# Squared-ReLU MLP by seven products: where the factors' differences, one weight sum and the last pair's stores are made

## The chip, the cores and the metric

The kernel runs on one core of a Trainium2 chip. The metric is device time of one launch in microseconds (us), lower is better; the time of a kernel is the median of its runs. The engines are named as the profile names them: PE (TensorE, matmuls), DVE (VectorE), ACT (ScalarE), POOL (GpSimd) and SP (SyncE, which only issues DMAs here). Each takes its instructions in the order of the program that was built; an instruction whose input isn't ready holds what is behind it on its engine.

## The reference

One layer on x (512 × 2048, float32): RMSNorm, a combined projection, stick-breaking attention and a gated branch, a merge, then the MLP, to which everything here belongs:

```
x = x + out
x = x + W2 relu(W1 RMSNorm(x))^2      # W1: 2048 x 8192, W2: 8192 x 2048
```

The result is float32 and is compared as such. The kernel makes a float32 product of three matmuls: each factor is split into a high part (hi, a cast by ACT) and the rest (lo = source − hi, a subtraction by DVE), and hi·hi, hi·lo and lo·hi are added in PSUM (`mm3`, L71 to L73).

## The kernel before

**First product.** The normalised x, turned (x2T, 16 tiles of 128 × 512), meets W1 in 32 pairs of 2 × 128 hidden columns. Pairs 0 and 1 are plain (`PLAIN = 2`). Pairs 2 to 31 take two blocks of columns, two halves of the tokens and two halves of the contraction as 2 × 2 blocks, and make seven products in place of eight (`NAMES` = y11, y21, m7, m6, y22, m4, m5, in this order). The seven factors of the activation side are x2T's own quarters (y11, y21, y22) and the differences m7 = y12 − y22, m6 = m7 − y11, m4 = y21 + m6, m5 = y11 − y12, made for each of eight k by `factors` (L646 to L649) while pair 1 runs, each into a new tile `m`, then split (L106, L107) into tiles `ys`. The weight side's sums are made for each pair by `Sums` on DVE: L172 (m7: w11 + w21), L176 (m6: + w22), L178 (y22: w12 is added). m5's factor w21 + w22 is made by a DMA that GpSimd issues and that adds w22 from DRAM into w21 (L174). SP loads the four blocks, 512 KB each (L166). Each product has 24 matmuls of 128 × 256, each pair 168.

**Hidden values.** `keep_hidden` squares a pair's activations, makes the same four differences from them, splits the seven factors and stores them to DRAM (`store`, 256 KB each, L687, by SP). The two plain pairs and pair 2 are kept together behind pair 2, then one pair behind each pair.

**Second product.** Eight chunks f of four pairs; for each chunk two halves g of the output columns; in each half seven products of 2 × 12 matmuls of 128 × 512 (i = 0 and 1 are two sets of weight blocks with their own `Sums`). GpSimd fetches the factors back (`ys<-store`, L737) and the residual (x2, from `kept`, 16 tiles, L754). The result of each product is added to x2 by DVE (L768). The next chunk's factors are fetched in `between`, behind each product.

**What sets the order.** The program is written as above, and a scheduler that models the engines (a `TileContext` with `schedule_with_timeline_sim=True`) sets the order of each engine's instructions. Tiles come from pools: `slots` (64 tiles of 256 KB) for activations and factors, `raws` for weight blocks (6) with `more` (6) added for the second product, and `w_piece` (6) for hi and lo of weights, which is three products ahead. `issue_after` holds an instruction behind another one in the order. `behind` is a list of small tasks; `step()` runs the next of them, `flush()` the rest. GpSimd and SP have eight transfers each in flight: an issue waits for the one eight earlier to land.

## Time and profile before

| | |
|---|---|
| median of 3 runs | 2529.33 us (2528.76 to 2530.37) |
| profiled execution | 2529.15 us |
| its span in the profile | 2527.2 us |
| PE busy | 2486.2 us, 98% of the span |
| DVE busy | 1600.5 us, 63% |
| pairs 0 and 1, then pair 2 | pair 2 from 1271.06 to 1301.0 us |
| pairs 3 to 30 | 1301.0 to 1865.5 us |
| pair 31 and the second product | 1865.5 us to the last matmul's end at 2521.9 us |

A row of the timeline has the start in us, the duration, the engine, the line of the kernel, the operation, the written tile and the read ones, and in brackets the idle time of the engine ahead of it with what ended it. A row of the table of stretches has the bounds, their length, then for each engine the busy time with the number of instructions, the granted clock of TensorE (1.00 is full), the share of DMA time and GB/s. Rows of waits have: total us, times, longest.

### The profile page before, as it was taken

Reading aid. Unit: us, or ns where it says so; the run is one execution under the profiler, and the core shown is the slowest. Engines: PE = TensorE matmul, PEld = TensorE weight load, DVE = VectorE, ACT = ScalarE, POOL = GpSimd, SP = SyncE. Lnnn points to the kernel's source line nnn. Section 1 sums busy time; section 2 is a strip of 40 time slices with the busy share of each in tenths; the row PEclk is TensorE's granted clock in tenths of the full one; section 3 lists DMA queues with packets and bytes.
Section 4 is the critical chain, followed back from the end, with each engine's and each line's share of the span. In section 5 each row is a group of like instructions: output and inputs, shape, how many; then the busy total and the mean of one; then the engine's idle time right before and its main releaser. Section 6 shows DMA issues by size and latency. Waiting matters only on the chain.

```text
span 2527.2 us, 35103 instructions
## 1 busy us (share of the span) xinstructions
PE 2486.2 (98%) x13658; PEld 2170.2 (86%) x13658; DVE 1600.5 (63%) x2106; ACT 1036.0 (41%) x1510; POOL 336.7 (13%) x425
## 2 busy tenths in 40 slices
PE   8999999999999999999999999999988999999999
PEld 7888888888888888888889999999986888888887
DVE  4555463232335343332798888888877889889887
ACT  5333342222223322232466666666653333333333
POOL 0212110000121010100000000000033223222210
PEclk9999999999999999999999999999998999999999
DMA  5332322333433233344368888887899787777763
GB/s 175 92 84 75 92 67 92 100 96 97 117 93 108 92 96 120 117 158 125 85 185 220 229 227 223 220 223 214 221 313 332 248 257 248 223 215 221 248 183 94
DMA packets 324711, 418.62 MB, mean 166 GB/s; under 512 B 17040, under 2 KB 177856, under 8 KB 324544
## 3 DMA queue, kind: packets, MB, share of 16 engines
q1 hardware_dynamic: 265440, 320.94, 39.9%
q0 software_dynamic: 59104, 95.44, 15.9%
q8 instruction: 107, 1.75, 0.3%
q14 instruction: 60, 0.49, 0.1%
HBM read 349.20 MB, written 67.11 MB: 165 GB/s over the span
## 4 chain that ended last, share of the span: by engine, by line
PE 95%; DMA 2%; DVE 2%; issue 1%; ACT 1%; POOL 0%; SPq 0%; DVEq 0%; POOLq 0%; ACTq 0%
PE q L72 17%; PE q L71 17%; PE q L73 17%; PE xo L73 2%; PE xo L71 2%; PE xo L72 2%; PE gb L71 2%; PE gb L72 2%; PE gb L73 2%; PE ga L71 2%; PE ga L72 2%; PE ga L73 2%; DMA w_raw<-in_w_ff_dram 2%; PE v L71 1%; PE v L73 1%; PE v L72 1%
## 5 line engine op out<-in xcount | busy, mean ns | idle before, releaser
L106 ACT CAST w_hi<-w_raw 128x1024 fp32r<-128x1024 f32 x434 | 456.8, 1052 | 600.7 <-PE q L72 548.8
L95 DVE TENSOR_TENSOR w_lo<-w_raw,w_hi 128x1024 fp32r<-128x1024 f32 x216 | 268.1, 1241 | 597.2 <-ACT w_hi L93 593.0
L107 DVE TENSOR_TENSOR w_lo<-w_raw,w_hi 128x1024 fp32r<-128x1024 f32 x434 | 530.6, 1223 | 137.4 <-ACT w_hi L106 137.1
L93 ACT CAST w_hi<-w_raw 128x1024 fp32r<-128x1024 f32 x216 | 227.2, 1052 | 664.9 <-PE ga L72 99.6
L72 PE MATMUL q<-ys,w_hi 128*128 128x256 f32 x1680 | 476.4, 284 | 4.1 <-DVE ys L107 4.1
L73 PE MATMUL q<-ys,w_lo 128*128 128x256 f32 x1680 | 472.7, 284 | 6.4 <-DVE w_lo L107 6.4
L71 PE MATMUL q<-ys,w_hi 128*128 128x256 f32 x1680 | 476.7, 285 | 1.0 <-ACT ys L106 0.8
L72 PE MATMUL q<-w_lo,ys 128*128 128x512 f32 x896 | 351.3, 392 | 11.1 <-DVE w_lo L107 11.1
L73 PE MATMUL q<-w_hi,ys 128*128 128x512 f32 x896 | 350.8, 392 | 0.0
L72 PEld LDWEIGHTS q<-ys,w_hi 128*128 128x128 f32 x1680 | 324.5, 193 | 4.9 <-DVE ys L107 4.9
L73 PEld LDWEIGHTS q<-ys,w_lo 128*128 128x128 f32 x1680 | 322.4, 193 | 6.6 <-DVE w_lo L107 6.6
L71 PEld LDWEIGHTS q<-ys,w_hi 128*128 128x128 f32 x1680 | 324.5, 193 | 1.9 <-ACT ys L106 1.5
L71 PE MATMUL q<-w_hi,ys 128*128 128x512 f32 x896 | 315.3, 391 | 0.9 <-ACT w_hi L106 0.9
L72 PEld LDWEIGHTS q<-w_lo,ys 128*128 128x128 f32 x896 | 169.6, 189 | 47.5 <-DVE w_lo L107 12.2
L71 PEld LDWEIGHTS q<-w_hi,ys 128*128 128x128 f32 x896 | 169.5, 189 | 36.6 <-ACT w_hi L106 1.3
L73 PEld LDWEIGHTS q<-w_hi,ys 128*128 128x128 f32 x896 | 169.6, 189 | 35.4
L174 POOL DMA_DIRECT2D w_raw<-in_w_ff_dram x62 | 85.9, 1393 | 819.2 <-DVE w_raw L172 543.6
L768 DVE TENSOR_TENSOR x<-x,q 128x512 f32<-128x512 f32 x256 | 167.9, 682 | 9.0 <-PE q L73 7.3
L737 POOL DMA_DIRECT2D ys<-store x224 | 126.8, 599 | 208.0 <-PE q L73 173.1
L71 PE MATMUL xo<-w_hi,mT_hi 128*128 128x512 f32 x256 | 100.5, 393 | 0.0
L73 PE MATMUL xo<-w_hi,mT_lo 128*128 128x512 f32 x256 | 99.9, 391 | 0.0
L72 PE MATMUL xo<-w_lo,mT_hi 128*128 128x512 f32 x256 | 99.7, 389 | 0.0
(259 smaller groups left out, 4216.2 us busy)
## 6 DMA issues: line engine op xcount, KB each, us to landing
w_raw<-in_w_ff_dram SPq DMA_DIRECT2D x256, 512.0 KB, 5.2
w_raw<-in_w_in_dram SPq DMA_DIRECT2D x144, 512.0 KB, 3.8
store<-ys SPq DMA_DIRECT2D x224, 256.0 KB, 5.1
ys<-store POOLq DMA_DIRECT2D x224, 256.0 KB, 6.0
w_raw<-in_w_ff_dram POOLq DMA_DIRECT2D x62, 512.0 KB, 6.9
w_raw<-in_w_out_dram SPq DMA_DIRECT2D x32, 512.0 KB, 3.8
w_raw<-in_w_oa_dram SPq DMA_DIRECT2D x16, 512.0 KB, 3.7
w_raw<-in_w_ob_dram SPq DMA_DIRECT2D x16, 512.0 KB, 3.7
```

The lines of the kernel that those rows point to most:

```text
L71: nc.tensor.matmul(o, lhsT=lh[0], rhs=rh[0], start=start, stop=False, **kw)
L72: nc.tensor.matmul(o, lhsT=lh[0], rhs=rh[1], start=False, stop=False, **kw)
L73: nc.tensor.matmul(o, lhsT=lh[1], rhs=rh[0], start=False, stop=stop, **kw)
L93: nc.scalar.copy(out=hi, in_=raw)
L95: nc.vector.tensor_tensor(out=lo, in0=raw, in1=f32(hi), op=ALU.subtract)
L106: nc.scalar.copy(out=hi, in_=src)
L107: state["lo"] = nc.vector.tensor_tensor(out=lo, in0=src, in1=f32(hi), op=ALU.subtract)
L174: nc.gpsimd.dma_start(out=self.w21, in_=self.blocks[1, 1], accum_op=ALU.add)
L737: nc.gpsimd.dma_start(out=f32(t), in_=store[f][NAMES.index(name), p])
L768: nc.vector.tensor_tensor(out=a, in0=a, in1=o, op=op)
```

## The change

- `factors` becomes `factor`, which makes one kind of difference for one k, and writes it in place, into x2T's y22 (m7, m6, m4) or y12 (m5). Pair 1's four steps make m7 for all eight k, then m6 for all eight; m4 and m5 of the first k are made ahead of pair 2, those of the others as tasks in `behind`, two k at a time, behind the products of pair 2.
- The kept pairs: one behind pair 2, up to two behind each later pair until none is left over, in place of all at once.
- `Sums` has `loaded=False` for pair 31 and for chunk f = 0 (`strassen_tokens` with `loaded=f > 0`): w21 + w22 is then an addition on DVE (L181 in the new numbering) ahead of m5, and there is no accumulating DMA.
- The fetches of chunk 0 (L788 in the new numbering) and of x2 (L803) are written mixed: three factors ahead of the second product, the others behind its products, with two tiles of x2 at a time; the fetches of chunk 1 begin at the end of f = 0, g = 0.
- f = 0, g = 0 has its m7 sums held behind the last addition to pair 31's activations (`issue_after`).
- Pair 31's squares, differences, splits and stores are tasks of `behind` in f = 1 (`keeping`).

```diff
     class Sums:
-        def __init__(self, blocks, tiles):
-            self.blocks = blocks
+        def __init__(self, blocks, tiles, loaded=True):
+            self.blocks, self.loaded = blocks, loaded
...
         def parts(self, name):
...
                 nc.vector.tensor_tensor(out=self.a, in0=self.w11, in1=self.w21, op=ALU.add)
-                nc.gpsimd.dma_start(out=self.w21, in_=self.blocks[1, 1], accum_op=ALU.add)
+                if self.loaded:
+                    nc.gpsimd.dma_start(out=self.w21, in_=self.blocks[1, 1], accum_op=ALU.add)
...
                 nc.vector.tensor_tensor(out=self.w12, in0=self.c, in1=self.w12, op=ALU.add)
+            if name == "m5" and not self.loaded:
+                nc.vector.tensor_tensor(out=self.w21, in0=self.w21, in1=self.w22, op=ALU.add)
...
-    def strassen_columns(wap, c0, rhs, evac):
+    def strassen_columns(wap, c0, rhs, evac, loaded=True):
...
             evac(name, o)
+            step()
...
-    def strassen_tokens(wap, r0, c0, lhs, evac, between):
+            step()
+    def strassen_tokens(wap, r0, c0, lhs, evac, between, loaded=True, after=None):
...
             for i in range(2):
-                hi, lo = ws[i].parts(name)
+                with tc.issue_after(after.ins) if after and name == "m7" else nullcontext():
+                    hi, lo = ws[i].parts(name)
...
             between(name)
+            step()
...
 -    def factors(ys, act, k):
+    def factor(ys, act, k, name):
         y11, y12, y21, y22 = act[0][:, :HS], act[0][:, HS:], act[1][:, :HS], act[1][:, HS:]
-        ta, tb = slot("m"), slot("m")
-        m = {"m7": ta[:, :HS], "m6": ta[:, HS:], "m4": tb[:, :HS], "m5": tb[:, HS:]}
-        nc.vector.tensor_tensor(out=m["m7"], in0=y12, in1=y22, op=ALU.subtract)
-        nc.vector.tensor_tensor(out=m["m6"], in0=m["m7"], in1=y11, op=ALU.subtract)
-        nc.vector.tensor_tensor(out=m["m4"], in0=y21, in1=m["m6"], op=ALU.add)
-        nc.vector.tensor_tensor(out=m["m5"], in0=y11, in1=y12, op=ALU.subtract)
-        for name in ("m7", "m6", "m4", "m5"):
-            ys[name, k] = halves(m[name])
+        o, in0, in1, op = {"m7": (y22, y12, y22, ALU.subtract), "m6": (y22, y22, y11, ALU.subtract),
+                           "m4": (y22, y21, y22, ALU.add), "m5": (y12, y11, y12, ALU.subtract)}[name]
+        nc.vector.tensor_tensor(out=o, in0=in0, in1=in1, op=op)
+        ys[name, k] = halves(o)
 ...
+    def keeping(p, act):
+        ys = {}
+        def keep(name):
+            if name == "y11":
+                for a in act:
+                    nc.scalar.activation(out=a, in_=a, func=AF.Square)
+            if name in ("y11", "y21", "y22"):
+                h = act[name[1] == "2"]
+                ys[name, 0] = halves(h[:, :HS] if name[2] == "1" else h[:, HS:])
+            else:
+                factor(ys, act, 0, name)
+            nc.sync.dma_start(out=store[p // GROUP][NAMES.index(name), p % GROUP], in_=f32(ys[name, 0]))
+        return [lambda name=name: keep(name) for name in ("y11", "y21", "y22", "m7", "m6", "m4", "m5")]
...
             if p == PLAIN - 1:
-                for k in range(kt // 2, kt // 2 + 2):
-                    factors(hs, x2T[2 * k:2 * k + 2], k)
+                for i in range(kt, kt + 4):
+                    factor(hs, x2T[i % 8 * 2:i % 8 * 2 + 2], i % 8, "m7" if i < 8 else "m6")
...
         acts.append(act)
-    rhs = {name: [sides(hs[name, k]) for k in range(KT // 2)] for name in NAMES}
+    def last_factors(k):
+        for name in ("m4", "m5"):
+            factor(hs, x2T[2 * k:2 * k + 2], k, name)
+    class Late:
+        def __init__(self, name):
+            self.name = name
+        def __getitem__(self, k):
+            return sides(hs[self.name, k])
+    rhs = {name: Late(name) for name in NAMES}
+    last_factors(0)
+    def two(k):
+        last_factors(k)
+        if k + 1 < KT // 2:
+            last_factors(k + 1)
+    behind.extend([lambda k=k: two(k) for k in range(1, KT // 2, 2)])
     def hidden(p):
...
                           "m5": [(a22, ALU.subtract), (a12, ALU.add)]}.get(name, []):
-                nc.vector.tensor_tensor(out=a, in0=a, in1=o, op=op)
-        strassen_columns(w_ff1[0], p * 2 * P, rhs, evac)
+                state["evac"] = nc.vector.tensor_tensor(out=a, in0=a, in1=o, op=op)
+        strassen_columns(w_ff1[0], p * 2 * P, rhs, evac, loaded=p < pairs - 1)
...
     pairs = DFF // (2 * P)
-    for p in range(PLAIN, pairs):
+    for p in range(PLAIN, pairs - 1):
         acts.append(hidden(p))
-        if p == pairs - 1:
-            lhs = {name: fetch(0, name) for name in NAMES}
-        while acts:
+        flush()
+        for _ in range(min(len(acts), 1 if p == PLAIN else 2)):
             keep_hidden(p + 1 - len(acts), acts.pop(0))
+    act = hidden(pairs - 1)
+    def residual(half, t, c):
+        tb, j = 2 * half + t, c
+        x2[tb, j] = slot("x2")
+        nc.gpsimd.dma_start(out=x2[tb, j], in_=kept[tb, j])
+    lhs = {}
+    def fetch_first(name):
+        lhs[name] = fetch(0, name)
+        if name in ("y11", "m7", "m6", "y22"):
+            half, c = {"y11": (0, 0), "m7": (1, 1), "m6": (0, 1), "y22": (1, 0)}[name]
+            for t in range(2):
+                residual(half, t, c)
+    for name in NAMES[:3]:
+        fetch_first(name)
...
     state["more"] = ctx.enter_context(tc.tile_pool(name="more", bufs=6))
-    for tb in range(NTB):
-        for j in range(D // W):
-            t = slot("x2")
-            nc.gpsimd.dma_start(out=t, in_=kept[tb, j])
-            x2[tb, j] = t
...
         ahead = {}
+        if f == 1:
+            behind.extend(keeping(pairs - 1, act))
...
             def evac_y(name, t, o):
...
             def between(name):
-                i = NAMES.index(name) + g * 5
-                if f < chunks - 1 and (i < 5 if g == 0 else i < 7):
+                i = NAMES.index(name)
+                if f == 0:
+                    if g == 0 and i + 3 < len(NAMES):
+                        fetch_first(NAMES[i + 3])
+                    for half, c in {(0, "m4"): [(0, 2)], (1, "y11"): [(1, 3)], (1, "y21"): [(0, 3)],
+                                    (1, "m7"): [(1, 2)]}.get((g, name), []):
+                        for t in range(2):
+                            residual(half, t, c)
+                    i = i - 6 if g == 0 else i + 1
+                    asked = 0 <= i < len(NAMES)
+                else:
+                    i += g * 5
+                    asked = i < (5 if g == 0 else 7)
+                if f < chunks - 1 and asked:
                     ahead[NAMES[i]] = fetch(f + 1, NAMES[i])
-            strassen_tokens(w_ff2[0], f * GROUP * 2 * P, g * 2 * W, lhs, evac_y, between)
+            strassen_tokens(w_ff2[0], f * GROUP * 2 * P, g * 2 * W, lhs, evac_y, between,
+                            loaded=f > 0, after=None if f or g else state["evac"])
```

The order of DVE where pair 1 ends and pair 2 begins, before (`ys` are factors' low halves, `m` the differences' tiles, `w_lo` with number 9407 that of pair 2's m7):

```order
L646 TENSOR_TENSOR m_9154<-x2T_8328,x2T_8365 128x256
L649 TENSOR_TENSOR m_9155<-x2T_8328 128x256
L107 TENSOR_TENSOR ys_9094<-m_9083,ys_9094 128x256
L107 TENSOR_TENSOR ys_9097<-m_9083,ys_9097 128x256
L107 TENSOR_TENSOR w_lo_9407<-w_raw_9338,w_hi_9406 128x1024
L647 TENSOR_TENSOR m_9154<-m_9154,x2T_8328 128x256
L107 TENSOR_TENSOR w_lo_9438<-w_raw_9339,w_hi_9437 128x1024
L648 TENSOR_TENSOR m_9155<-x2T_8365,m_9154 128x256
L107 TENSOR_TENSOR ys_9160<-m_9154,ys_9160 128x256
L107 TENSOR_TENSOR ys_9163<-m_9154,ys_9163 128x256
```

The same engine in the new order, where m7's last factors are split (the first low half of pair 2's weights is 9273):

```order
L107 TENSOR_TENSOR ys_9045<-x2T_8365,ys_9045 128x256
L107 TENSOR_TENSOR ys_9049<-x2T_8439,ys_9049 128x256
L107 TENSOR_TENSOR ys_9053<-x2T_8594,ys_9053 128x256
L107 TENSOR_TENSOR ys_9057<-x2T_8608,ys_9057 128x256
L655 TENSOR_TENSOR x2T_8069<-x2T_8069,x2T_8032 128x256
L655 TENSOR_TENSOR x2T_8143<-x2T_8143,x2T_8106 128x256
L95 TENSOR_TENSOR w_lo_9182<-w_raw_9178,w_hi_9180 128x1024
L655 TENSOR_TENSOR x2T_8365<-x2T_8365,x2T_8328 128x256
L655 TENSOR_TENSOR x2T_8439<-x2T_8439,x2T_8402 128x256
L107 TENSOR_TENSOR ys_9115<-x2T_7773,ys_9115 128x256
L655 TENSOR_TENSOR x2T_8594<-x2T_8594,x2T_8587 128x256
L655 TENSOR_TENSOR x2T_8608<-x2T_8608,x2T_8601 128x256
```

Before, the m7 factor of the sixth k was still to be made after the low half of pair 2's m7 weights; now all m7 factors stand ahead of the last low half of the plain pairs' weights (9182), and m6's differences are under way there.

DVE where pair 31 ends and the second product begins, before. 17006 is pair 31's w21 and 17197 the low half of its m5 weights; 17356 to 17361 are the buffers of the second product's first weights with i = 0 (w11, w12, w21, w22, and the sums of m7 and m6), 17366 to 17371 those with i = 1:

```order
L172 TENSOR_TENSOR w_raw_17370<-w_raw_17366,w_raw_17368 128x1024
L725 TENSOR_TENSOR relu_17002<-relu_17002,q_17048 128x256
L172 TENSOR_TENSOR w_raw_17360<-w_raw_17356,w_raw_17358 128x1024
L107 TENSOR_TENSOR w_lo_17197<-w_raw_17006,w_hi_17196 128x1024
L176 TENSOR_TENSOR w_raw_17371<-w_raw_17370,w_raw_17369 128x1024
L107 TENSOR_TENSOR w_lo_17379<-w_raw_17356,w_hi_17378 128x1024
L176 TENSOR_TENSOR w_raw_17361<-w_raw_17360,w_raw_17359 128x1024
L725 TENSOR_TENSOR relu_17003<-relu_17003,q_17080 128x256
L107 TENSOR_TENSOR w_lo_17395<-w_raw_17366,w_hi_17394 128x1024
```

The new order of the same place, from two rows behind the low half of pair 31's m5 weights (17181) on; 17248 to 17253 are the buffers with i = 0, 17258 to 17263 those with i = 1:

```order
L776 TENSOR_TENSOR relu_16987<-relu_16987,q_17063 128x256
L107 TENSOR_TENSOR w_lo_17287<-w_raw_17258,w_hi_17286 128x1024
L776 TENSOR_TENSOR relu_16987<-relu_16987,q_17002 128x256
L776 TENSOR_TENSOR relu_16986<-relu_16986,q_17002 128x256
L173 TENSOR_TENSOR w_raw_17252<-w_raw_17248,w_raw_17250 128x1024
L173 TENSOR_TENSOR w_raw_17262<-w_raw_17258,w_raw_17260 128x1024
L107 TENSOR_TENSOR w_lo_17319<-w_raw_17249,w_hi_17318 128x1024
L177 TENSOR_TENSOR w_raw_17253<-w_raw_17252,w_raw_17251 128x1024
L181 TENSOR_TENSOR w_raw_17250<-w_raw_17250,w_raw_17251 128x1024
L177 TENSOR_TENSOR w_raw_17263<-w_raw_17262,w_raw_17261 128x1024
L181 TENSOR_TENSOR w_raw_17260<-w_raw_17260,w_raw_17261 128x1024
L107 TENSOR_TENSOR w_lo_17335<-w_raw_17259,w_hi_17334 128x1024
```

Before, the m7 and m6 sums of the second product stood ahead of and among the low halves of pair 31's m5 and of y11; now they stand behind both and behind pair 31's last additions, and the low half of y21 for i = 1 (17335) stands behind both m6 sums and both new additions.

SP around the loads of the second half of f = 0, before (numbers from 17672 on are weight blocks of g = 1; 17286 to 17310 are pair 31's factors):

```order
L166 DMA w_raw_17672<-in_w_ff2_dram 128x2x512
L166 DMA w_raw_17682<-in_w_ff2_dram 128x2x512
L166 DMA w_raw_17673<-in_w_ff2_dram 128x2x512
L687 DMA store7_8743<-ys_17286 128x512
L687 DMA store7_8743<-ys_17289 128x512
L687 DMA store7_8743<-ys_17292 128x512
L166 DMA w_raw_17683<-in_w_ff2_dram 128x2x512
L687 DMA store7_8743<-ys_17301 128x512
L687 DMA store7_8743<-ys_17304 128x512
L166 DMA w_raw_17674<-in_w_ff2_dram 128x2x512
```

SP at the same place in the new order:

```order
L167 DMA w_raw_17576<-in_w_ff2_dram 128x2x512
L167 DMA w_raw_17586<-in_w_ff2_dram 128x2x512
L167 DMA w_raw_17577<-in_w_ff2_dram 128x2x512
L167 DMA w_raw_17587<-in_w_ff2_dram 128x2x512
L167 DMA w_raw_17578<-in_w_ff2_dram 128x2x512
L167 DMA w_raw_17588<-in_w_ff2_dram 128x2x512
```

The stores of pair 31's factors are gone from between the loads. Ahead of these rows the eight loads of g = 0 and the seven stores of pair 30 have the same places in both orders; in the new one the seventh load is w21 with i = 0 (17250) and the eighth w22 with i = 0 (17251).

More of the change, by code (lines that the diff above doesn't have):

```diff
@@ L190, in strassen_columns @@
                   for h in range(2) for c in range(2)}
-        w = Sums(blocks, [state["raw"].tile([P, KH, P], F32, name="w_raw", tag="w_raw") for _ in range(6)])
+        w = Sums(blocks, [state["raw"].tile([P, KH, P], F32, name="w_raw", tag="w_raw") for _ in range(6)],
+                 loaded)
         banks = {}
@@ L212, in strassen_tokens @@
             pool = (state["raw"], state["more"])[i]
-            ws.append(Sums(blocks, [pool.tile([P, KQ, W], F32, name="w_raw", tag="w_raw") for _ in range(6)]))
+            ws.append(Sums(blocks, [pool.tile([P, KQ, W], F32, name="w_raw", tag="w_raw") for _ in range(6)],
+                           loaded))
         banks = {}
@@ L682, in keep_hidden @@
         ys = {}
-        for name, src in (("y11", act[0][:, :HS]), ("y21", act[1][:, :HS]), ("y22", act[1][:, HS:])):
-            ys[name, 0] = halves(src)
-        factors(ys, act, 0)
-        for i, name in enumerate(NAMES):
-            nc.sync.dma_start(out=store[p // GROUP][i, p % GROUP], in_=f32(ys[name, 0]))
+        y11, y12, y21, y22 = act[0][:, :HS], act[0][:, HS:], act[1][:, :HS], act[1][:, HS:]
+        for name, src in (("y11", y11), ("y21", y21), ("y22", y22)):
+            ys[name] = halves(src)
+        ta, tb = slot("m"), slot("m")
+        m = {"m7": ta[:, :HS], "m6": ta[:, HS:], "m4": tb[:, :HS], "m5": tb[:, HS:]}
+        nc.vector.tensor_tensor(out=m["m7"], in0=y12, in1=y22, op=ALU.subtract)
+        nc.vector.tensor_tensor(out=m["m6"], in0=m["m7"], in1=y11, op=ALU.subtract)
+        nc.vector.tensor_tensor(out=m["m4"], in0=y21, in1=m["m6"], op=ALU.add)
+        nc.vector.tensor_tensor(out=m["m5"], in0=y11, in1=y12, op=ALU.subtract)
+        for name in ("m7", "m6", "m4", "m5"):
+            ys[name] = halves(m[name])
+        for i, name in enumerate(NAMES):
+            nc.sync.dma_start(out=store[p // GROUP][i, p % GROUP], in_=f32(ys[name]))
+    def keeping(p, act):
[11 more added lines that the diff above has]
+        return [lambda name=name: keep(name) for name in ("y11", "y21", "y22", "m7", "m6", "m4", "m5")]
     PLAIN = 2
```

1 line of the change is left out of this document (removed).

## The prediction

> **What bounds the kernel now.** I began with the page's first part, then the waits of TensorE.
>
> ```profile
> PE 2486.2 (98%) x13658; PEld 2170.2 (86%) x13658; DVE 1600.5 (63%) x2106; ACT 1036.0 (41%) x1510; POOL 336.7 (13%) x425
> ```
> ```profile
> PE q L72 <- DVE w_lo L107: 11.1, 3, 5.4
> PE q L73 <- DVE w_lo L107: 6.4, 1, 6.4
> ...
> PE q L72 <- DVE ys L107: 4.1, 3, 1.6
> ```
>
> TensorE sets the end: it is busy for 98% of the span. A change that removes no matmul can win only what TensorE idles, or runs at half clock, beside the changed code. The named waits add to some 22 us, but they leave the half clock out. The table of stretches gives both: matmuls that write q alone, from the first Strassen pair on, cut where the pairs of the first product begin (1301.0 is the second one, 1865.5 the last) and where the second product has settled.
>
> ```profile
> 1271.06:1301.00 29.94, 24.90 (x168) 23.14 (x168) 0.83 (x2) 1.55 (x4) 0.83 0.51 134
> 1301.00:1865.50 564.50, 564.50 (x4706) 564.50 (x4705) 44.25 (x112) 39.27 (x112) 1.00 0.84 226
> 1865.50:1896.80 31.30, 24.89 (x183) 23.92 (x181) 1.16 (x3) 1.41 (x4) 0.89 1.03 393
> 1896.80:1960.00 63.20, 51.22 (x198) 40.96 (x198) 12.78 (x21) 0.00 (x0) 0.86 0.97 327
> 1960.00:2036.00 76.00, 76.00 (x337) 62.92 (x336) 20.93 (x32) 0.00 (x0) 1.00 0.75 235
> 2036.00:2521.90 485.90, 485.90 (x2144) 402.03 (x2142) 133.92 (x204) 0.00 (x0) 1.00 0.69 212
> ```
>
> The second row is the norm: 28 pairs of 168 matmuls in 564.5 us, 20.16 us a pair, without a gap. The first pair took 29.94, so place A loses 29.94 − 20.16 = 9.8 us. The last row gives 485.9 / 2144 = 0.2266 us a matmul; the second product's 2688 need 609.2 us. From 1865.5 to 2521.9 the kernel takes 656.4 us for one pair and the second product, which need 20.2 + 609.2 = 629.4. Place B loses 27.0 us, all before 1960. The rest of TensorE's losses lie in stages that the change doesn't touch. So the change can win 36.8 us and no more: the floor is 2529.3 − 36.8 = 2492.5.
>
> Place A: TensorE's share and clock, and three of its rows (the last bracket is the idle time and what ended it).
>
> ```profile
> 1280.00:1284.00 4.00, 1.43 (x4) 0.93 (x5) 3.97 (x13) 2.22 (x7) 0.00 (x0) 0.74 0.45 131
> 1284.00:1288.00 4.00, 2.50 (x8) 1.65 (x8) 4.00 (x13) 2.74 (x9) 0.00 (x0) 0.50 0.00 0
> 1288.00:1292.00 4.00, 4.00 (x21) 4.00 (x21) 3.99 (x8) 4.00 (x12) 0.00 (x0) 0.50 0.15 55
> ```
> ```profile
> 1280.85 0.39 PE L72 MATMUL q<-ys,w_hi 128*128 128x256 f32 x1 [1.63 <-DVE ys L107]
> ...
> 1283.66 0.58 PE L72 MATMUL q<-ys,w_hi 128*128 128x256 f32 x1 [1.12 <-DVE ys L107]
> ...
> 1286.34 0.58 PE L72 MATMUL q<-ys,w_hi 128*128 128x256 f32 x1 [1.33 <-DVE ys L107]
> ```
>
> VectorE is full, and TensorE waits for m7's factors one k at a time, since before makes m7, m6, m4 and m5 of each k together. TensorE's small gaps also bring the clock to 0.50 until 1292.
>
> Place B has three long waits. Each is a low half of a weight (w_lo) which stands, in VectorE's order, behind a sum of weights that waits for a load.
>
> ```profile
> 1883.54 1.23 DVE L172 TENSOR_TENSOR w_raw<-w_raw 128x1024 f32<-128x1024 f32 x1 [6.33 <-DMA w_raw<-in_w_ff_dram]
> ...
> 1887.18 1.22 DVE L172 TENSOR_TENSOR w_raw<-w_raw 128x1024 f32<-128x1024 f32 x1 [2.08 <-issue]
> 1888.32 1.22 DVE L107 TENSOR_TENSOR w_lo<-w_raw,w_hi 128x1024 fp32r<-128x1024 f32 x1
> 1890.61 1.23 DVE L176 TENSOR_TENSOR w_raw<-w_raw 128x1024 f32<-128x1024 f32 x1 [1.07 <-DMA w_raw<-in_w_ff_dram]
> ...
> 1899.08 1.23 DVE L176 TENSOR_TENSOR w_raw<-w_raw 128x1024 f32<-128x1024 f32 x1 [6.11 <-DMA w_raw<-in_w_ff_dram]
> ...
> 1900.55 1.22 DVE L107 TENSOR_TENSOR w_lo<-w_raw,w_hi 128x1024 fp32r<-128x1024 f32 x1
> ...
> 1941.26 1.22 DVE L172 TENSOR_TENSOR w_raw<-w_raw 128x1024 f32<-128x1024 f32 x1 [4.76 <-DMA w_raw<-in_w_ff_dram]
> ```
> ```profile
> 1889.59 0.58 PE L73 MATMUL q<-ys,w_lo 128*128 128x256 f32 x1 [6.41 <-DVE w_lo L107]
> ...
> 1901.82 0.80 PE L72 MATMUL q<-w_lo,ys 128*128 128x512 f32 x1 [4.92 <-DVE w_lo L107]
> 1918.58 0.50 PE L71 MATMUL q<-w_hi,ys 128*128 128x512 f32 x1 [0.91 <-ACT w_hi L106]
> 1919.84 0.52 PE L72 MATMUL q<-w_lo,ys 128*128 128x512 f32 x1 [0.76 <-DVE w_lo L107]
> 1943.68 0.80 PE L72 MATMUL q<-w_lo,ys 128*128 128x512 f32 x1 [5.39 <-DVE w_lo L107]
> ```
>
> The loads are late because the DMA engines are full (share 1.03 above). What they carry from 1855 to 1960:
>
> ```profile
> DMA packets 16367, 35.71 MB, mean 340 GB/s; under 512 B 1796, under 2 KB 3844, under 8 KB 16361
> ...
> ys<-store POOLq DMA_DIRECT2D x54, 256.0 KB, 7.7
> w_raw<-in_w_ff_dram SPq DMA_DIRECT2D x18, 512.0 KB, 15.2
> ...
> x<-kept POOLq DMA_DIRECT2D x16, 256.0 KB, 8.1
> w_raw<-in_w_ff_dram POOLq DMA_DIRECT2D x5, 512.0 KB, 9.1
> ```
>
> I split B's 27.0. From 1865.5 to 1896.8 there are a pair and 15 matmuls of the second product, which need 20.16 + 15 × 0.2266 = 23.6 of the 31.3 us: B1 = 7.7, of it 6.4 the wait itself. The rest, B2 = 19.3, has 4.9 + 0.9 + 0.8 + 5.4 = 12.0 of waits, which leaves 7.3 for half clock behind three stops. I use 2.4 us as the price of a stop in the clock.
>
> **Place A, by parts.** The 32 differences are the same in number and size, and so are their splits; only their places move. 16 of them (m7, m6) go into the stretch of the two plain pairs, the other 16 behind products of the first Strassen pair, two k at a time. m7's factors then stand in VectorE's order well ahead of the product that reads them, and the waits of 0.2 to 1.6 us go, with their half clock: +9.8.
>
> Two things come back. The plain pairs run under a VectorE that is nearly full already (14.23 of 15 us; the 128x256 operations there are 0.42 us, and start about 0.33 apart where they queue, as 1900.22 does ahead of 1900.55):
>
> ```profile
> 1225.00:1240.00 15.00, 15.00 (x119) 15.00 (x119) 14.23 (x31) 8.13 (x20) 0.00 (x0) 0.92 0.13 37
> ...
> 1900.22 0.41 DVE L725 TENSOR_TENSOR relu<-relu,q 128x256 f32<-128x256 f32 x1
> ```
>
> 16 × 0.33 = 5.3 us more work for VectorE there. The bounds are 0 (all covered, since the next stretch has slack) and 5.3 + 2.4. I take 0.5, near the low end: only the low halves of the first plain pair's third weight piece stand behind it, and TensorE reaches it a little later. Secondly, the new order puts the third pair's first matmuls ahead of the second pair's last product; their w_hi cast can't start until m4 gives its buffer back, and takes 1.05 us:
>
> ```profile
> L106 ACT CAST w_hi<-w_raw 128x1024 fp32r<-128x1024 f32 x434 | 456.8, 1052 | 600.7 <-PE q L72 548.8
> ```
>
> That is one stop of about 0.9, bounds 0 and 0.9 + 2.4; I take 0.9 + 1.4, as it is a short one. A wins 9.8 − 0.5 − 2.3 = 7.0, bounds 9.8 and −1.2.
>
> Keeping two pairs per step instead of three at once moves work inside stretches where TensorE never waited (second row of the table). Nothing.
>
> **Place B, by parts.** B1: f = 0, g = 0 now holds its first sums behind the last pair's last addition (issue_after on m7), so the last pair's m5 has its low half with nothing waiting for a load in front of it. 7.7 us go; none would if the held sums stood in VectorE's order ahead of it all the same. I take 7.7, for the order has them behind.
>
> The start of the second product. The same eight loads stand in SP's queue in the same places, after the same stores. Before, the seventh and eighth are waited for at 1890.61 and 1899.08, 25.1 and 33.6 us after the last pair's start. GpSimd's stream of 28 factors, 16 pieces of x2 and the next factors has the same length, only mixed in another order, and is limited by free slots as before. So I leave the landings there. In the new order the seventh is w21 of i = 0 and the eighth w22 of i = 0. VectorE then has: sum m7 i0 (waits for the seventh), sum m7 i1, low half of y21 i0, then sum m6 i0 (waits for the eighth), L181, sum m6 i1, L181, low half of y21 i1. At 1.14 us from start to start (1887.18 to 1888.32), y21 i0 is ready at 25.1 + 3 × 1.14 + 0.1 = 28.6. TensorE ends the pair at 20.2 and y11's 24 matmuls at 20.2 + 5.4 = 25.6: a stop of 3.0. Its 12 matmuls and the half clock end at 28.6 + 2.7 + 2.4 = 33.7. y21 i1 is ready at 33.6 + 5 × 1.14 + 0.1 = 39.4: 5.7, of which some 0.6 is filled by m7 matmuls that the order puts ahead; 5.1. The two stops cost 3.0 + 5.1 + 2 × 2.4 = 12.9. L181's two operations (2.3 us) are part of this.
>
> The third stop (1943.68) goes. Before, its load stands in SP's queue between stores of the last pair's factors, and these are now stored in f = 1; the five accumulating DMAs are gone from the full stretch too (5 × 512 KB read, and the buffers they held). The second half's loads start as m7's sums free the buffers, about 26 us, and are asked for only after 38 us more of matmuls. So B2 wins 19.3 − 12.9 = 6.4. If the eighth load came 11 us sooner and the seventh 3, both stops would vanish (19.3); if the eighth comes 6 us later, nothing is won.
>
> Work added later: f = 0 has four sums on VectorE (4.6 us), f = 1 the last pair's seven splits and four differences (11 × 0.33 = 3.7).
>
> ```profile
> 1960.00:2036.00 76.00, 76.00 (x337) 62.92 (x336) 67.17 (x74) 29.55 (x28) 20.27 (x32) 1.00 0.75 235
> ```
>
> With 67.2 of 76 us a chunk has 8.8 spare, more than either; the cover is thin in one half-chunk. I take 0, and 3.7 + 2.4 if it fails.
>
> Sum: 7.0 + 7.7 + 6.4 = 21.1. The profiled execution took 2529.15 (1.95 around its span of 2527.2), the median is 2529.33: 2508.
>
> [...]
>
> **The rivals.** *Token start clean:* bytes that left the full stretch (2.6 MB of accumulating reads and 1.8 MB of stores, of 35.7) let the two late loads land in time. At 340 GB/s that is 13 us of traffic, but most of it lay behind 1899. Then A 7.0 and B 27.0 go: 2495.
>
> *The wait only moves:* B1 goes, but the loads are no earlier and VectorE now has five operations between the eighth load and a low half that TensorE needs at once. B2 stays at 19.3, A wins only 4: 2529.3 − 7.7 − 4 = 2517.6.
>
> *Slower: the eighth load starves.* Half of the bytes there are GpSimd's stream, 62 transfers of 256 KB in the new order; of these two rows of GpSimd the second is the ninth issue after the first:
>
> ```profile
> 1881.07 0.54 POOL L737 DMA_DIRECT2D ys<-store  x1 [0.25 <-PE q L73]
> ...
> 1891.12 0.54 POOL L737 DMA_DIRECT2D ys<-store  x1 [0.49 <-DMA ys<-store]
> ```
>
> At 1.1 us each the stream lasts 68 us. Each us that w22 of i = 0 lands after 33.6 costs a us, as everything behind sum m6 waits. It decides from 33.6 + 21.1 = 55 us on; at the stream's end (some 73 us) the loss is 39 − 21 = 18: 2547. Against it: before, the same place in the queue landed at 33.6 beside the same stream.
>
> *The change doesn't do what it says:* the factors can't come sooner since VectorE is full (14.23 of 15), and the added 5.3 + 2.4 eats A; the loads decide B as before, the first wait reappearing at y21: within 0.2%, 2528.
>
> **Chances.** My sum 0.50; clean start 0.19; the wait moves 0.21; no change 0.05; slower 0.05. The likeliest case itself spans 2502 to 2513. The range leaves out the far part of the clean start and everything above the moved wait: 2495.5 to 2518. A measurement tells 0.2% (5 us) from no change. Faster 0.90, same 0.05, slower 0.05.
>
> **What would show it.** Between 1278 and 1292 no wait on ys; the first Strassen pair takes 20 to 24 us. The last pair takes 20.2 us with no wait of L73. Then two waits on w_lo, of 3 and 5 us, 25 and 34 us after the last pair's start, each ended by VectorE behind an L173 or L177 which a load ended; none 38 us later. The second product from f = 1 on without a gap at 76 us a chunk. It is wrong if the accumulated loads land at other times (the token start tells), if a wait on w_lo appears in the plain pairs, or if f = 1 shows stops behind the splits of the last pair.

## The result, and the profile after

The changed kernel takes 2508.59 us (median of 4 runs, 2508.14 to 2509.51) against 2529.85 for the kernel before in the same comparison. The ratio is 0.9916, 95% interval 0.9899 to 0.9933. The forecast was 2508 with a range of 2495.5 to 2518. The profiled execution took 2509.51 us, 19.6 less than the profiled one of before.

The waits of TensorE in the changed kernel (total us, times, longest):

```profile
PE q L72 <- DVE w_lo L107: 10.7, 4, 7.6
...
PE q L71 <- ACT w_hi L106: 0.8, 1, 0.8
PE f L73 <- DVE w_lo L95: 0.4, 1, 0.4
```

The table of stretches of the changed kernel, matmuls into q alone, cut where its pair 2 ends (1293.22), its pair 31 begins (1857.70) and its last matmul ends (2502.36):

```profile
1270.00:1293.22 23.22, 20.41 (x168) 20.32 (x169) 0.85 (x2) 1.51 (x4) 1.00 0.45 117
1293.22:1857.70 564.48, 564.48 (x4706) 564.48 (x4705) 44.23 (x112) 39.36 (x112) 1.00 0.85 229
1857.70:1886.00 28.30, 28.30 (x206) 26.78 (x205) 2.33 (x6) 1.40 (x4) 1.00 0.98 355
1886.00:1912.00 26.00, 18.40 (x71) 14.67 (x70) 5.39 (x8) 0.00 (x0) 0.80 1.04 395
1912.00:1940.00 28.00, 25.07 (x108) 19.61 (x107) 6.39 (x10) 0.00 (x0) 1.00 0.71 249
...
2112.00:2502.36 390.36, 390.36 (x1723) 323.01 (x1721) 107.88 (x165) 0.00 (x0) 1.00 0.66 201
```

**Place A.** Pair 2's first matmul starts at 1271.99, so the pair takes 1293.22 − 1271.99 = 21.2 us; before it took 29.9. The wait on ys is gone. What is left is one stop of 0.82 at a cast (w_hi) and one of 0.40 in the plain pairs (the last row of the waits above):

```profile
1290.73 0.39 PE L71 MATMUL q<-ys,w_hi 128*128 128x256 f32 x1 [0.82 <-ACT w_hi L106]
```

The plain pairs are 0.9 us longer than before (their first matmul starts at 1222.89, before at 1222.72). From there to the end of pair 2 are 70.3 us in place of 78.3: A wins 8.0 us.

**Place B.** From 1857.70 to 2502.36 are 644.7 us for work that needs 629.4: a loss of 15.3, where before lost 27.0. B wins 11.7. Pair 31 has no stop (third row: TensorE busy for the whole 28.30). VectorE and TensorE at the start of the second product:

```profile
1879.95 2.36 DVE L173 TENSOR_TENSOR w_raw<-w_raw 128x1024 f32<-128x1024 f32 x2 [1.13 <-DMA w_raw<-in_w_ff_dram]
1882.22 1.22 DVE L107 TENSOR_TENSOR w_lo<-w_raw,w_hi 128x1024 fp32r<-128x1024 f32 x1
1888.95 1.23 DVE L177 TENSOR_TENSOR w_raw<-w_raw 128x1024 f32<-128x1024 f32 x1 [5.51 <-DMA w_raw<-in_w_ff_dram]
1890.10 1.22 DVE L181 TENSOR_TENSOR w_raw<-w_raw 128x1024 f32<-128x1024 f32 x1
1891.23 1.22 DVE L177 TENSOR_TENSOR w_raw<-w_raw 128x1024 f32<-128x1024 f32 x1
1892.37 1.22 DVE L181 TENSOR_TENSOR w_raw<-w_raw 128x1024 f32<-128x1024 f32 x1
1893.50 1.22 DVE L107 TENSOR_TENSOR w_lo<-w_raw,w_hi 128x1024 fp32r<-128x1024 f32 x1
...
1922.49 1.23 DVE L181 TENSOR_TENSOR w_raw<-w_raw 128x1024 f32<-128x1024 f32 x1 [1.40 <-DMA w_raw<-in_w_ff_dram]
```
```profile
1894.78 0.80 PE L72 MATMUL q<-w_lo,ys 128*128 128x512 f32 x1 [7.60 <-DVE w_lo L107]
1926.04 0.50 PE L72 MATMUL q<-w_lo,ys 128*128 128x512 f32 x1 [1.66 <-DVE w_lo L107]
1927.77 0.72 PE L71 MATMUL q<-w_hi,ys 128*128 128x512 f32 x2 [0.29 <-DVE x L832]
1930.64 0.50 PE L72 MATMUL q<-w_lo,ys 128*128 128x512 f32 x1 [0.98 <-DVE w_lo L107]
```

The order is the predicted one, row by row: the seventh load ends L173's wait, the eighth ends L177's, and the low half of y21 with i = 1 comes behind L177, L181, L177, L181. But the loads came at 22.2 and 31.2 us after pair 31's start, not at 25.1 and 33.6, so the first stop didn't appear and the second, alone, is 7.6. Three short stops, 2.9 us together, appear 67 to 73 us after pair 31's start, where I had none. The fourth of the L72 waits in the list above is a stop of 0.45 at 2045.72, where the chunk f = 2 begins.

Together A and B win 19.7 us in the profile, which is the 19.6 between the profiled executions; the medians are 21.3 apart.

### The profile page after: what moved, and what is told of

Its sections match the earlier page's. It is cut to its first block, busy times and chain, and to the rows that moved or that the text cites. A ratio compares the mean times of both kernels' runs of the same rounds, so it can differ in the third digit from the quotient of the medians.

```text
span 2507.8 us, 35108 instructions
## 1 busy us (share of the span) xinstructions
PE 2477.8 (99%) x13658; PEld 2163.2 (86%) x13658; DVE 1603.1 (64%) x2111; ACT 1034.0 (41%) x1510; POOL 329.5 (13%) x420
## 4 chain that ended last, share of the span: by engine, by line
PE 94%; DMA 2%; DVE 2%; issue 1%; ACT 1%; POOL 0%; SPq 0%; DVEq 0%; POOLq 0%
PE q L72 17%; PE q L73 16%; PE q L71 16%; PE xo L73 2%; PE xo L71 2%; PE xo L72 2%; PE gb L71 2%; PE gb L73 2%; PE gb L72 2%; PE ga L71 2%; PE ga L72 2%; PE ga L73 2%; DMA w_raw<-in_w_ff_dram 1%; PE v L71 1%; PE v L73 1%; PE v L72 1%
## 5 line engine op out<-in xcount | busy, mean ns | idle before, releaser
L71 PE MATMUL q<-ys,w_hi 128*128 128x256 f32 x1680 | 474.0, 283 | 0.8 <-ACT w_hi L106 0.8
L72 PE MATMUL q<-ys,w_hi 128*128 128x256 f32 x1680 | 473.9, 283 | 0.0
L72 PE MATMUL q<-w_lo,ys 128*128 128x512 f32 x896 | 350.5, 391 | 10.7 <-DVE w_lo L107 10.7
L71 PEld LDWEIGHTS q<-ys,w_hi 128*128 128x128 f32 x1680 | 322.5, 192 | 1.0 <-ACT w_hi L106 1.0
L72 PEld LDWEIGHTS q<-ys,w_hi 128*128 128x128 f32 x1680 | 322.5, 192 | 0.0
L71 PE MATMUL q<-w_hi,ys 128*128 128x512 f32 x896 | 313.7, 390 | 0.3 <-DVE x L832 0.3
L72 PEld LDWEIGHTS q<-w_lo,ys 128*128 128x128 f32 x896 | 168.9, 189 | 47.9 <-DVE w_lo L107 13.0
L71 PEld LDWEIGHTS q<-w_hi,ys 128*128 128x128 f32 x896 | 168.5, 188 | 35.8 <-DVE x L832 0.7
L175 POOL DMA_DIRECT2D w_raw<-in_w_ff_dram x57 | 79.4, 1393 | 773.7 <-DVE w_raw L173 461.3
L788 POOL DMA_DIRECT2D ys<-store x224 | 124.6, 566 | 244.9 <-PE q L73 186.8
L71 PE MATMUL xo<-w_hi,mT_hi 128*128 128x512 f32 x256 | 100.5, 393 | 0.0
L72 PE MATMUL xo<-w_lo,mT_hi 128*128 128x512 f32 x256 | 99.7, 389 | 0.0
```

The costliest lines, as they stand in the source:

```text
L71: nc.tensor.matmul(o, lhsT=lh[0], rhs=rh[0], start=start, stop=False, **kw)
L72: nc.tensor.matmul(o, lhsT=lh[0], rhs=rh[1], start=False, stop=False, **kw)
L175: nc.gpsimd.dma_start(out=self.w21, in_=self.blocks[1, 1], accum_op=ALU.add)
L788: nc.gpsimd.dma_start(out=f32(t), in_=store[f][NAMES.index(name), p])
```

## The experiments

Below, t is the time from pair 31's start. In the profile of the changed kernel that is 567.0 us behind the stop of 0.82 in pair 2 (1290.73), and in the others it is set by the same distance. The kernel before has pair 31's start at 1865.5. The expectations count from a point 1.0 us later: their 21.2 and 30.2 are 22.2 and 31.2 here. Each time is a median; the ratio to the kernel before has its interval with it. The runs were made in three rounds, in which the kernel before took 2529.24 to 2529.95 us, so a difference of less than 1 us from the changed kernel says nothing.

**One part alone.** The kernel before with `factor`, `Late`, `two` and a `step()` behind each product of a pair; nothing else.

```diff
+    rhs = {name: Late(name) for name in NAMES}
+    last_factors(0)
+    behind.extend([lambda k=k: two(k) for k in range(1, KT // 2, 2)])
...
         acts.append(hidden(p))
+        flush()
...
         while acts:
             keep_hidden(p + 1 - len(acts), acts.pop(0))
```

> The kernel before with only the first part: differences one kind at a time and in place, m4 and m5 behind the products of the first Strassen pair. The plain pairs' results are still all kept behind that pair. Theory (the factors alone stalled the first Strassen pair, and the two places are independent): that pair takes 21 to 22 us in place of 29.9, the last pair and the second product stay as before: 2529.9 - 8.5 = 2521.4 (2519 to 2524). Rival (three pairs kept at once need the room on VectorE that the moved differences now take): a stop of VectorE's splits in the third pair, 2524 to 2528.

Measured: 2529.3 us, ratio 0.9998 (0.9989 to 1.0008). Nothing is won. TensorE's rows:

```profile
1290.61 0.39 PE L71 MATMUL q<-ys,w_hi 128*128 128x256 f32 x1 [0.82 <-ACT w_hi L106]
1309.95 0.58 PE L71 MATMUL q<-ys,w_hi 128*128 128x256 f32 x1 [5.17 <-ACT relu L753]
...
1889.53 0.58 PE L73 MATMUL q<-ys,w_lo 128*128 128x256 f32 x1 [7.59 <-DVE w_lo L107]
1902.76 0.79 PE L72 MATMUL q<-w_lo,ys 128*128 128x512 f32 x1 [5.79 <-DVE w_lo L107]
```

Pair 2 is as short as in the changed kernel (the 0.82 stop stands at the same place), but pair 3 has a stop of 5.2 us and its half clock (granted 0.68 in 1308 to 1312), at the evacuation that the keeping of three pairs delays. VectorE comes to the last m4 of the three kept pairs at 1308.45, before at 1309.67, so at nearly the same time, while pair 3 begins 8 us sooner. What is left of the gain is lost in place B: the stops are 7.6 and 5.8 us where they were 6.4 and 4.9, for TensorE comes sooner to the same late loads. The stop is the rival's; the time lies above both ranges, as neither counted the loss in place B.

**The keeping.** The changed kernel, with all pairs kept at once behind pair 2 again:

```diff
-        for _ in range(min(len(acts), 1 if p == PLAIN else 2)):
+        for _ in range(len(acts)):
```

> The changed kernel, but the plain pairs and pair 2 are kept all at once behind pair 2, as before. Theory (after a_alone: the moved differences win 8.4 us in the first Strassen pair only if the keeping is spread, since VectorE cannot do three pairs' keeping beside pair 3's weights): a stop of some 5 us by L709's relu or what stands behind it in pair 3 and its half clock: 2508.6 + 7 = 2515.5 (2514 to 2517). Rival (what a_alone lost was lost in place B): 2509.

Measured: 2517.69 us, ratio 0.9952 (0.9937 to 0.9967): 9.1 us more than the changed kernel. The four runs lie between 2515.2 and 2519.7; the profiled one took 2516.0.

```profile
1308.92 0.58 PE L71 MATMUL q<-ys,w_hi 128*128 128x256 f32 x1 [5.30 <-ACT relu L773]
```

The same stop in pair 3 again. So the moved differences pay only together with the spread keeping; I had put the spreading at nothing.

**No hold.** The changed kernel without `issue_after` on the first m7 sums.

```diff
-                            loaded=f > 0, after=None if f or g else state["evac"])
+                            loaded=f > 0)
```

> The changed kernel without the hold of the second product's first m7 sums behind the last pair's last addition. Prediction as on record (the hold is what removes the stop of 6.4 us in the last pair, 7.7 with the clock): 2516, with L73 waiting in the last pair again. Theory from the new order: the load that m5's low half now stands behind is the fifth, which lands before TensorE needs that low half, so no stop in the last pair; y11 i0 stands behind the seventh load (21.2 us after the last pair's start) and y11 i1 behind the eighth (30.2): two stops of 3 to 4 us and their half clock, some 12 us in place of 10: 2511 (2509 to 2513).

Measured: 2510.73 us, ratio 0.9924 (0.9909 to 0.9939). VectorE's fifth load and TensorE's stops:

```profile
1871.82 1.23 DVE L173 TENSOR_TENSOR w_raw<-w_raw 128x1024 f32<-128x1024 f32 x1 [2.75 <-DMA w_raw<-in_w_ff_dram]
```
```profile
1881.59 0.50 PE L72 MATMUL q<-w_lo,ys 128*128 128x512 f32 x1 [3.42 <-DVE w_lo L107]
1891.60 0.80 PE L72 MATMUL q<-w_lo,ys 128*128 128x512 f32 x1 [6.04 <-DVE w_lo L107]
```

The hold is worth some 2 us here, not 7.7. Without it no stop comes back in pair 31, as the fifth load lands at t = 14.4 and the sum on it stands in front of m5's low half early enough; before, the sum on the same place in the queue started at 1883.54, t = 18.0.

**The accumulating DMA.** w21 + w22 by DMA again, for pair 31 and f = 0 (`loaded=True`).

```diff
-        strassen_columns(w_ff1[0], p * 2 * P, rhs, evac, loaded=p < pairs - 1)
+        strassen_columns(w_ff1[0], p * 2 * P, rhs, evac)
...
-                            loaded=f > 0, after=None if f or g else state["evac"])
+                            after=None if f or g else state["evac"])
```

> The changed kernel with w21 + w22 made by the accumulating DMA again, for the last pair and for f = 0. Theory (the additions on VectorE stand between the eighth load and a low half, 1.14 us each): the stop of 7.6 us gets 2.3 shorter, but 2.6 MB of reads come back into a stretch that is full, and the buffer of w21 is free later, so a load of the second half is late: 2506 without that, up to 2514 with it; I expect 2511. Rival (the additions are free and the bytes decide): the seventh and eighth load land 3 us or more later than 21.2 and 30.2, 2515.

Measured: 2510.52 us, ratio 0.9921 (0.9906 to 0.9936), 1.9 more than the changed kernel, and:

```profile
1892.01 2.36 DVE L177 TENSOR_TENSOR w_raw<-w_raw 128x1024 f32<-128x1024 f32 x2 [8.35 <-DMA w_raw<-in_w_ff_dram]
```

The eighth load lands at t = 33.7, as before (33.6), and not at 31.2. So the accumulating DMAs are what made the eighth load late by 2.4 us. Which of them, and how, the run doesn't tell: GpSimd issues pair 31's at 1851.90, ahead of the loads, after a wait of 18.6 us that holds its fetches back as well, and the two of g = 0 at 1885.06, also ahead of the landing. For the seventh load the run shows nothing, since its order has the sixth and the seventh exchanged. The additions, which add 2 × 1.14 us behind the eighth load, give about that much back: this swap alone is nearly even at the start of the second product.

**The last pair's stores.** Pair 31 kept right away, as before:

```diff
-    act = hidden(pairs - 1)
+    keep_hidden(pairs - 1, hidden(pairs - 1))
...
-        if f == 1:
-            behind.extend(keeping(pairs - 1, act))
```

> The changed kernel with the last pair kept at the start of the second product, as before. Theory: eleven short operations (11 x 0.33 us, and the first of them longer) stand on VectorE between the eighth load and y21's low half with i = 1, and seven stores stand in SP's queue ahead of the loads of the second half: the stop of 7.6 grows by 4, and a stop of about 5 and its half clock comes back some 70 us after the last pair's start: 2508.6 + 4 + 5 = 2518 (2514 to 2521). Rival (the late store does nothing): 2509.

Measured: 2523.87 us, ratio 0.9975 (0.9966 to 0.9985): 15.3 us more than the changed kernel, and more than the theory's 9. SP's queue and TensorE's stops:

```profile
1880.70 2.35 SPq L167 DMA_DIRECT2D w_raw<-in_w_ff_dram  x2
1893.51 5.49 SPq L700 DMA_DIRECT2D store<-ys  x7
1902.52 57.52 SPq L167 DMA_DIRECT2D w_raw<-in_w_ff_dram  x11
```
```profile
1897.82 0.79 PE L71 MATMUL q<-w_hi,ys 128*128 128x512 f32 x1 [11.34 <-ACT w_hi L106]
1899.08 0.79 PE L72 MATMUL q<-w_lo,ys 128*128 128x512 f32 x1 [0.47 <-DVE w_lo L107]
1935.37 0.80 PE L72 MATMUL q<-w_lo,ys 128*128 128x512 f32 x1 [11.72 <-DVE w_lo L107]
```

The first stop grew by 4 as expected (ScalarE's casts of factors hold w_hi too). The other stop, 77 us after pair 31's start, is 11.7 us, not 5: seven stores stand ahead of six of the second half's eight loads. Without this part the rest of the change would win nothing in place B: 2529.85 − 8.0 for place A is 2521.9, and this kernel takes 2523.9.

**Order or loads?** Four runs on the stops that are left. First the order: m6's sums behind y21's low half and the additions behind m4's, in g = 0 alone, then also in g = 1 with its m7 sums behind m5's low half (the diff's last line, which only the second has).

```diff
+            hold = {"m7": after, "m6": lows.get("y21"), "m5": lows.get("m4")}.get(name) if after else None
             for i in range(2):
-                with tc.issue_after(after.ins) if after and name == "m7" else nullcontext():
+                with tc.issue_after(hold.ins) if hold else nullcontext():
                     hi, lo = ws[i].parts(name)
+                lows[name] = state["lo"]
...
+                            after=None if f else (state["lo"] if g else state["evac"]))
```

> The changed kernel with the m6 sums of f = 0, g = 0 held behind y21's last low half, and the w21 + w22 additions behind m4's. Same loads, same operations, another order on VectorE. Theory (the 7.6 us stop is an order in which a ready low half stands behind a late load): the stop and its half clock go, 7.6 + 2.6 = 10 us: 2498.5 (2496 to 2501). The three short stops at the end of the first half (1.7, 0.3, 1.0) stay. Rival (the loads themselves are too late, the wait moves to m6): TensorE waits for m6's low half instead, 2504 to 2509.

Measured: 2510.97 us, ratio 0.9925 (0.991 to 0.994). No gain.

```profile
1889.92 2.36 DVE L177 TENSOR_TENSOR w_raw<-w_raw 128x1024 f32<-128x1024 f32 x2 [4.29 <-DMA w_raw<-in_w_ff_dram]
...
1922.62 1.23 DVE L181 TENSOR_TENSOR w_raw<-w_raw 128x1024 f32<-128x1024 f32 x1 [2.50 <-DMA w_raw<-in_w_ff_dram]
```
```profile
1894.66 0.79 PE L72 MATMUL q<-w_lo,ys 128*128 128x512 f32 x1 [4.16 <-DVE w_lo L107]
...
1928.70 0.79 PE L72 MATMUL q<-w_lo,ys 128*128 128x512 f32 x1 [7.12 <-DVE w_lo L107]
```

The eighth load comes at t = 31.6, much as in the changed kernel; the stop of 7.6 is now 4.2, at m6, and the next half pays: its additions wait for loads in front of m5's low half, a stop of 7.1. The rival (the wait moves to m6) holds; the time lies above its range as well, because of the stop of 7.1, which was in neither of the two outcomes.

> As hold_first_half, and the sums of g = 1 held likewise: m7's behind the low half of m5 of the first half, m6's behind y21's, the additions behind m4's. Theory: the short stops of 3 us go too: 2495.5 (2493 to 2498). Rival (they come from VectorE being full there, not from its order): 2498.5, stops of about 1 us at other operations.

Measured: 2503.01 us, ratio 0.9894 (0.9878 to 0.9911), 5.6 us below the changed kernel. The stops at the end of the first half are gone. This is left, and a stop of 0.91 us at a w_hi cast 110 us after pair 31's start:

```profile
1893.33 0.79 PE L72 MATMUL q<-w_lo,ys 128*128 128x512 f32 x1 [4.20 <-DVE w_lo L107]
```

So the short stops were VectorE's order and not its being full. If the 4.2 us are the load itself, they go when it lands sooner (below, under *Together*). The theory missed mostly by those 4.2 and their half clock (granted 0.88 in 1886 to 1900).

Then the loads. Pair 30's seven stores behind all eight loads:

```diff
+        if "put" in state:
+            with tc.issue_after(ws[0].last.ins), tc.issue_after(ws[1].last.ins):
+                state.pop("put")()
```

> The changed kernel with pair 30's seven stores put behind all eight loads in SP's queue. Theory (loads are served in the queue's order, some 3.5 us for 512 KB while all is full): the eighth load lands about 5 us sooner than 30.2 us after the last pair's start, the seventh as before; the stop of 7.6 shrinks to 2.6, 2508.6 - 5 = 2503.5 (2501 to 2506). Rival (GpSimd's stream sets when it lands, not the stores): 2508.

Measured: 2509.14 us, ratio 0.9918 (0.9903 to 0.9933).

```profile
1884.68 1.23 DVE L177 TENSOR_TENSOR w_raw<-w_raw 128x1024 f32<-128x1024 f32 x1 [0.18 <-DMA w_raw<-in_w_ff_dram]
...
1915.38 1.23 DVE L173 TENSOR_TENSOR w_raw<-w_raw 128x1024 f32<-128x1024 f32 x1 [5.43 <-DMA w_raw<-in_w_ff_dram]
```
```profile
1890.50 0.50 PE L72 MATMUL q<-w_lo,ys 128*128 128x512 f32 x1 [2.25 <-DVE w_lo L107]
1921.52 0.80 PE L72 MATMUL q<-w_lo,ys 128*128 128x512 f32 x1 [5.32 <-DVE w_lo L107]
```

The landing went as the theory said: t = 26.4, 4.8 sooner, and the stop is 2.3. But the second half's first sum (L173) now waits 5.4 us for its load, whose queue has all seven stores between it and the eighth load, and TensorE stops for 5.3 us there. The time was moved and not saved.

GpSimd's stream stopped until the last pair's activations are done (the product of the two tiles is used by nothing; the later pieces of x2 and the fetches of chunk 1 wait for it in the same way):

```diff
     for name in NAMES[:3]:
         fetch_first(name)
+    gate = nc.gpsimd.tensor_tensor(out=slot("gate"), in0=act[0], in1=act[1], op=ALU.mult)
...
-                        fetch_first(NAMES[i + 3])
+                        with tc.issue_after(gate.ins):
+                            fetch_first(NAMES[i + 3])
...
```

> The changed kernel with GpSimd's stream stopped after the first three kinds of factors and four pieces of x2, until the last pair's activations are done (a product of the two activation tiles that nothing uses, on GpSimd, stands ahead of the rest). Theory (the loads are late because the stream takes its share of the DMA engines): about 8 transfers of 256 KB less before 20 us, the eighth load lands 4 us or more sooner than 30.2, 2504 (2500 to 2506), unless a factor of m6 is then late. Rival (stores or the loads' own rate decide): 2508; with late factors 2512 or more, with TensorE waiting for a DMA of ys.

Measured: 2504.55 us, ratio 0.9899 (0.9885 to 0.9914).

```profile
1888.73 0.50 PE L72 MATMUL q<-w_lo,ys 128*128 128x512 f32 x1 [1.91 <-DVE w_lo L107]
1892.19 0.50 PE L72 MATMUL q<-w_lo,ys 128*128 128x512 f32 x1 [0.88 <-DVE w_lo L107]
...
1921.55 0.50 PE L72 MATMUL q<-w_lo,ys 128*128 128x512 f32 x1 [3.82 <-DVE w_lo L107]
```

VectorE's sums no longer wait for a load at the start of the second product: the one on the eighth load starts at t = 25.5, without a wait. Stops of 1.9 and 0.9 us are left there, and 3.8 at the end of the first half. TensorE waits for no fetched factor. So what is left of the loads' lateness comes from the stream's head start.

**Together.** The holds of both halves with the gate, with the later stores, and with both.

> hold_both_halves and stream_gated together. Theory (the stop of 4.2 us that hold_both_halves leaves is the eighth load itself, and the gate brings it some 5 us sooner): no stop over 1 us at the start of the second product: 2503.0 - 4.2 - 2.4 = 2496.5 (2495 to 2499). Rival (the gate's gain and the holds' are the same time): 2502 to 2503.

Measured: 2497.42 us, ratio 0.9872 (0.9857 to 0.9887): 11.2 us less than the changed kernel, as the theory said; the 4.2 us were the load. One stop of 0.4 us is left at the start of the second product:

```profile
1894.42 0.50 PE L72 MATMUL q<-w_lo,ys 128*128 128x512 f32 x1 [0.36 <-DVE w_lo L107]
```

> hold_both_halves with pair 30's stores behind the eight loads. The eighth load lands about 5 us sooner (stores_later: 25.9 us after the last pair's start), so the stop of 4.2 us goes; the loads of g = 1 come later by the seven stores, but with the sums held behind m5's low halves they are asked for later as well. Theory: 2497 (2495 to 2500). Rival (as in stores_later, the time goes to a stop at the end of the first half): 2502 to 2504.

Measured: 2504.46 us, ratio 0.9901 (0.9886 to 0.9916), as the rival has it. The stop at m6 is down to 0.4 us, and two at the end of the first half take its place:

```profile
1921.85 0.74 PE L71 MATMUL q<-w_hi,ys 128*128 128x512 f32 x1 [2.52 <-DVE x L844]
1923.59 0.80 PE L72 MATMUL q<-w_lo,ys 128*128 128x512 f32 x1 [1.00 <-DVE w_lo L107]
```

> All three: holds in both halves, the gate on GpSimd's stream, pair 30's stores behind the loads. If either of the two alone takes the stop at m6 away, this adds nothing: 2496.5 (2495 to 2499), the same as holds_and_gate within 1 us. If the gated stream's factors or the later stores make a new stop, 2500.

Measured: 2496.75 us, ratio 0.9869 (0.9853 to 0.9886), the same as with holds and gate alone. The version with holds and gate beats both kernels, by a ratio of 0.9872 to the one before.

## Why the prediction was right, point by point

The time was right (2508 forecast, 2508.59 measured) and the likeliest case happened, but that it is so close is in part luck. In the profile the terms are 8.0, 7.7 and 4.0 where the sum had 7.0, 7.7 and 6.4: A was put 1.0 too low and B2 2.4 too high. Three steps below them were wrong: the spread keeping put at nothing, the landings left where they were, and the third stop gone.

*Place A, 7.0 us: 8.0 measured.* The loss in the plain pairs was put at 0.5 and is 0.9, of it 0.40 the stop. The stop of w_hi was put at 0.9 with 1.4 for the clock; it is 0.82, and the clock stays at 1.00, which is the difference.

*"Keeping two pairs per step ... Nothing."* This step is wrong. It is worth 9.1 us (three_at_once; 6.5 in the profiled executions), since without the 8.7 us that pair 2 lost TensorE reaches pair 3 with the keeping of three pairs still under way on VectorE. I read "TensorE never waited there" from a trace in which TensorE came 8 us later. The sum held only because the change did both.

*B1, 7.7 us by the hold.* The stop did go. But the hold is worth some 2 us here: no_hold, with the loads sooner, has no stop in pair 31. Nor has the kernel with the accumulating DMA, where the loads are as late as before and the hold is in place; a_alone, which has neither, has the stop. Either is enough.

*B2, a gain of 6.4.* B as a whole won 11.7, so with B1's 7.7 this term is 4.0. The row that failed is "So I leave the landings there": I counted most of the bytes that left as lying behind 1899, but with the accumulating DMAs back (`accumulated`) the eighth load lands at 33.7 again and not at 31.2. The seventh came 2.9 sooner than I had it, so the first stop (3.0) vanished; what made it sooner isn't shown. The second stop ended at t = 37.1, 2.3 sooner than the 39.4 worked out; the distance from load to low half, five operations at 1.14 us, was right. Two stops and their clock were to cost 12.9; one of 7.6 with half clock behind it (0.50 in 1896 to 1900) costs 26.0 − 71 × 0.2266 = 9.9 (the stretch 1886 to 1912).

*"The third stop goes."* It shrank from 5.4 to 2.9 in three pieces, and the clock stayed full. The stores' part of the argument was right, and larger than thought (kept_at_once: 11.7 us if they stay). The part that failed is the time at which the loads are asked for, put at 38 us of matmuls later: VectorE takes the additions at once, ahead of a low half that is needed sooner, and waits 1.40 us for a load there. With the sums held back (hold_both_halves) these stops are gone.

*"Work added later", taken as 0.* The stop of 0.45 at 2045.72 is all that appears behind the stores and splits that moved into f = 1. No run tests what made it.

*The rivals.* "Token start clean" didn't happen in the changed kernel and did in holds_and_gate, at 2497.4 where I had 2495. "The wait only moves" describes hold_first_half and stores_later well. The eighth load didn't starve: the stream does delay it, but in stream_gated, without the head start, it is only some 6 us sooner (25.5 or less, against 31.2).

*The price of a stop in the clock, 2.4.* It isn't flat. The stops of 0.82, 1.66 and 0.98 us in the changed kernel left the clock at 1.00, and the 1.4 behind the w_hi stop was nothing. The stop of 2.25 us in stores_later did cost clock: from 1891.36 to 1894.35 its matmuls start 0.43 us apart in place of 0.23. The stop of 3.0, which had a price of 2.4 in the sum, didn't come. The second stop did, and the price fits it: 9.9 − 7.6 = 2.3.

## What to carry to other kernels

An engine that takes instructions in order turns a late load into a stop for whatever stands behind the waiting instruction (here 5.51 us of VectorE waiting at L177 and 7.60 of TensorE); when a load can't be made sooner, put the operations that wait for it behind those that are needed first, and do it in the next stage as well, or the stop moves there (7.12 us in hold_first_half). A stretch without waits in the old trace is no proof that its work is free: it was free beside a stop that the same change removes, so cost each part with the stop gone (the spread keeping, put at nothing, is worth 9.1 us). When a stream of prefetches and loads that are needed soon share full DMA engines (share 1.04 in 1886 to 1912 of the changed kernel), try holding the stream back until those loads are nearly in: here it was stopped until t = 24.5, and the eighth load was in by 25.5.
